# A hybrid decoder layer on one core: writing a recurrence head's level preparation in one piece

## Chip, cores and metric

The kernel runs on one core of a Trainium2 chip. The metric is the device time of one execution in microseconds (us). Engines are named as in the profile: PE (TensorE matmuls), PEld (its weight loads), DVE (VectorE), ACT (ScalarE), POOL (GpSimd), SP (the queue that issues most DMAs).

## The reference, cut to what matters

One decoder layer over 2048 tokens of width 1024: modulated RMSNorm, one input projection, two head groups, an output projection, then a gated MLP with a short convolution. Head group A is sliding-window attention. Head group B, which the change touches, is a gated linear recurrence with 4 heads of key and value width 128:

```
f = lower_bound + (1 - lower_bound) * sigmoid(f_logit);  k = 1 - f;  q = silu(q)
S_t = diag(f_t) S_{t-1} + k_t i_t^T,   o_t = S_t^T q_t
```

In chunkwise form the score of query t and key s in a chunk is the sum over the key dimension of q_t times the product of f from s+1 to t times k_s.

## The kernel before

**Stages.** The mixer works through four groups g of 512 tokens (`GT`), the later stages through the output projection, the up projection and the down projection; the down projection starts at about 1970 us. In a group the four recurrence heads are handled in two pairs, (0, 1) and (2, 3). For each pair `hg_scores` (L781 to L884) builds the decayed scores AT of four chunks of 128 tokens, and `hg_state` (L886) carries the state. In the trace, `a_q` is a head's query tile, `K` its key tile, `f` its forget gate, all 128 x 512 float32, keys on partitions and tokens along the row.

**Levels.** A score between tokens that first differ in bit w of their index is a product of a scaled query and a scaled key. So `hg_scores` goes through widths w = 1, 2, 4, ... 64. `scaled(h, w)` (L819) multiplies the second halves of the query blocks by `tots` (for w = 1: f itself) and the first halves of the key blocks by it, and folds `tots` by two: three DVE instructions, written in place. Widths 0, 1 and 2 are done without matmuls over blocks: a DVE product (`raw`, L811, L816, L839) is split into a high part (ACT, to `ph` or `p`) and a low part (POOL, to `pl` or `p`), and much later summed by matmuls with a matrix of ones (`lv_d`, `lv<-ph`, `lv<-p`). From w = 4 on PE makes a block of scores (`lv<-a_q,K`) in a PSUM bank of the tag "hg" (two banks), and DVE or ACT merges it into AT.

**Preparation before the change.** For both heads of a pair: raw0 = q k, its split, q = q f, raw1 = odd q times even k, its split. Then for both heads: `scaled(h, 1)`, raw2, its split. Then for both heads: `scaled(h, 2)`. Then the loop over w = 4 to 64, again over both heads in each turn.

**Buffers.** The six `raw` tiles of a pair come from one tag, "ln", with `bufs=3`: three buffers, handed out in the order in which the tiles are written in the program. In the old order they are raw0 and raw1 of the first head, raw0 and raw1 of the second, raw2 of the first, raw2 of the second. A buffer is free again when both the ACT and the POOL instruction of its split are done.

**Order on the engines.** The program is fully unrolled. ACT is pinned to program order through `hg_scores` and `hg_state`. DVE, POOL, PE and SP are not pinned there: before the launch a planner places each engine's instructions by expected readiness, the earlier in the program the higher the priority. On the chip each engine then takes its list strictly in order. During the pair (0, 1) PE also has the projection `ps_i` of this group (`proj_i`), during the pair (2, 3) the attention projections `ps_k`, `ps_q` (`proj_attn`), so that level matmuls stand in PE's list between projection matmuls.

**Names in the rows.** `w_..h` and `w_..l` are high and low parts of projection weights, split by ACT and by DVE or POOL; `ada` and `part` belong to a sum over the conditioning weights that DVE does on the side; `s_q` is the sigmoid of a query, and POOL's `a_q<-a_q,s_q` makes silu. All rows show line L46, the helper through which every instruction passes.

Of the kernel before, what the change touches and what calls it, by code (L numbers as in the profile page):

```python
# [8 lines left out]
F32 = mybir.dt.float32  # L9
# [4 lines left out]
ALU = mybir.AluOpType  # L14
# [4 lines left out]
P = 128  # L19
# [6 lines left out]
GT = 512  # L26
# [27 lines left out]
def kernel(ctx, tc, x, c, ada_w, ada_b, mix_norm_g, w_in, b_in, attn_sinks, attn_out_g,  # L54
# [3 lines left out]
    V, S, G, TE, SY = (InOrder(tc, e) for e in (nc.vector, nc.scalar, nc.gpsimd, nc.tensor, nc.sync))  # L58
# [105 lines left out]
    def split(src, hi, lo, hi_eng=None, lo_eng=None):  # L164

        if hi_eng is V:
            V.tensor_copy(out=hi, in_=src)
        else:
            S.activation(hi, src, AF.Copy)
        (lo_eng or V).tensor_tensor(out=lo, in0=src, in1=hi.bitcast(F32), op=ALU.subtract)  # L170
# [59 lines left out]
    with ExitStack() as mx:  # L230
# [334 lines left out]
        for e in range(2):  # L565

            hp, op = slice(e * 64, e * 64 + 64), slice(64 - e * 64, 128 - e * 64)
# [4 lines left out]
        mt = hgp.enter_context(tc.tile_pool(name="mt", bufs=2, side="right", reuse_waits="tile"))  # L572
# [16 lines left out]
        for g in range(NG):  # L589
# [169 lines left out]
            qs, ks, fs, ats, on, kts, tots = {}, {}, {}, {}, {}, {}, {}  # L759
# [21 lines left out]
            def hg_scores(hs_):  # L781
# [11 lines left out]
                def sums(h, hi, lo, label):  # L793
# [4 lines left out]
                    TE.matmul(ps, lhsT=ones_r, rhs=lo, start=False, stop=True)  # L798
                    return ps


                ph, pl, p1 = {}, {}, {}
                for h in hs_:
# [11 lines left out]
                    raw = mt.tile([P, GT], F32, tag="ln", bufs=3, name=f"raw1_{g}_{h}")[:, 0:GT // 2]  # L815
                    V.tensor_tensor(out=raw, in0=q2[:, :, 1], in1=k2[:, :, 0], op=ALU.mult)  # L816
                    split(raw, p1[h][:, 0, :], p1[h][:, 1, :], lo_eng=G)

                def scaled(h, w):  # L819

                    q4 = qs[h].rearrange("p (n a h) -> p n a h", a=2, h=w)
                    k4 = ks[h].rearrange("p (n a h) -> p n a h", a=2, h=w)
                    t3 = tots[h].rearrange("p (n a) -> p n a", a=2)
                    ns = GT // (2 * w)
                    V.tensor_tensor(out=q4[:, :, 1, :], in0=q4[:, :, 1, :],
                                    in1=t3[:, :, 0:1].broadcast_to([P, ns, w]), op=ALU.mult)
                    V.tensor_tensor(out=k4[:, :, 0, :], in0=k4[:, :, 0, :],
                                    in1=t3[:, :, 1:2].broadcast_to([P, ns, w]), op=ALU.mult)
                    nt = mt.tile([P, ns], F32, tag=f"tot{w}", name=f"tot_{g}_{h}_{w}")
                    V.tensor_tensor(out=nt, in0=t3[:, :, 0], in1=t3[:, :, 1], op=ALU.mult)  # L830
                    tots[h] = nt

                for h in hs_:
                    scaled(h, 1)
                    q4 = qs[h].rearrange("p (n a h) -> p n a h", a=2, h=2)[:, :, 1, :]
                    k4 = ks[h].rearrange("p (n a h) -> p n a h", a=2, h=2)[:, :, 0, :]
                    raw = mt.tile([P, GT], F32, tag="ln", bufs=3, name=f"raw2_{g}_{h}")
                    full4 = [P, GT // 4, 2, 2]
                    V.tensor_tensor(out=raw.rearrange("p (n t s) -> p n t s", t=2, s=2),  # L839
                                    in0=q4.unsqueeze(3).broadcast_to(full4), in1=k4.unsqueeze(2).broadcast_to(full4),  # L840
                                    op=ALU.mult)
                    split(raw, ph[h][1], pl[h][1], lo_eng=G)
                for h in hs_:
                    scaled(h, 2)
                w = 4
                while w <= 64:
                    for h in hs_:
                        q, k, at = qs[h], ks[h], ats[h]
                        nm = f"{g}_{h}"
                        if w <= 16:  # L850
                            ps = full(h, w)
                        else:
                            ps = bank(f"lv_{nm}_{w}", "hg").rearrange("p (a b) -> p a b", a=4)
                            for cc in range(4):
                                for s0 in range(0, P, 2 * w):
                                    a0 = cc * P + s0
                                    TE.matmul(ps[s0:s0 + w, cc, s0 + w:s0 + 2 * w], lhsT=k[:, a0:a0 + w],
                                              rhs=q[:, a0 + w:a0 + 2 * w], start=True, stop=True)
                        scaled(h, w)
                        if w <= 16:  # L860
                            V.copy_predicated(at, bc4(lev[w]), ps)
                        else:
                            for s0 in range(0, P, 2 * w):
                                S.activation(at[s0:s0 + w, :, s0 + w:s0 + 2 * w],
                                             ps[s0:s0 + w, :, s0 + w:s0 + 2 * w], AF.Copy)
                    w *= 2
# [79 lines left out]
            weights(g, "i", 0, ahead=1)  # L946
            pin(True, S)
            hg_scores((0, 1))
            i_tok = proj_i()
            hg_state((0, 1))  # L950
# [9 lines left out]
            weights(g, "k", 0)  # L960
            pin(True, S)
            hg_scores((2, 3))
            hg_state((2, 3))
            pin(False, S)
# [561 lines left out]
```

## Time and profile before

| | |
|---|---|
| median of 3 runs | 2494.3 us (2492.16 to 2494.49) |
| the profiled execution | 2490.66 us |
| its span, first to last instruction | 2488.9 us |
| PE busy | 2323.8 us, 93% of the span |
| DVE busy | 1911.0 us, 77% |
| ACT busy | 1055.6 us, 42% |
| POOL busy | 919.4 us, 37% |
| mean granted TensorE clock | 0.974 |

Busy times are of the whole span. A row of the timeline gives the start in us from the span's start, the duration in us, engine, line, operation, output<-inputs, shape and type, the number of instructions merged into the row, and in brackets the engine's idle time before it and what ended it.

### The profile page before, as it was taken

How to read it: one execution, taken by the hardware profiler on the slowest of the kernel's cores; microseconds unless marked ns; L12 is line 12 of the kernel's file. 1: busy time of each engine (PE TensorE's matmuls, PEld its weight loads, DVE VectorE, ACT ScalarE, POOL GpSimd, SP SyncE). 2: the span in 40 equal slices, each digit the busy share in tenths (PEclk: the TensorE clock that was granted, in tenths of full speed). 3: DMA queues.
4: the chain of work that ended last, by engine and by line, in shares of the span. 5: the costliest groups of instructions: out<-in, count | busy, mean ns of one | idle time of the engine just before them, and what ended most of it. 6: DMA issues, size and time to landing. Idle time of an engine off the chain costs nothing.

```text
span 2488.9 us, 35680 instructions
## 1 busy us (share of the span) xinstructions
PE 2323.8 (93%) x13369; PEld 2010.0 (81%) x13369; DVE 1911.0 (77%) x2743; ACT 1055.6 (42%) x1776; POOL 919.4 (37%) x743
## 2 busy tenths in 40 slices
PE   5889898998989899999999999999999789997997
PEld 4778786887878688887888887788888679997997
DVE  8888778888876876568888888788877776676665
ACT  3336434623733454454333334333332344455443
POOL 6222212222322221225757564788888410011000
PEclk8999999999999999999999999999999889998999
DMA  7343233323322247664444245455454577687776
GB/s 213 90 119 98 81 91 96 94 69 101 95 68 85 85 159 246 204 204 131 139 129 144 93 140 189 158 159 163 161 157 166 199 260 218 211 283 263 260 243 203
DMA packets 337304, 389.90 MB, mean 157 GB/s; under 512 B 14069, under 2 KB 258763, under 8 KB 337131
## 3 DMA queue, kind: packets, MB, share of 16 engines
q1 hardware_dynamic: 326571, 347.25, 44.8%
q0 software_dynamic: 10560, 40.37, 4.4%
q8 instruction: 105, 1.72, 0.3%
q14 instruction: 68, 0.56, 0.1%
HBM read 293.71 MB, written 93.86 MB: 156 GB/s over the span
## 4 chain that ended last, share of the span: by engine, by line
PE 66%; DVE 13%; DMA 7%; POOL 6%; issue 5%; ACT 2%; SPq 0%; DVEq 0%; ACTq 0%; POOLq 0%
PE ps_u L46 24%; PE ps_d L46 15%; PE ps_o L46 5%; PE lv L46 3%; PE ps_hg L46 3%; PE ps_hq L46 2%; PE ps_hf L46 2%; PE ps_i L46 2%; PE att_o L46 2%; DVE ada L46 2%; DMA ada<-in_ada_w_dram 1%; POOL s L46 1%; PE ps_q L46 1%; DVE raw L46 1%; POOL sm L46 1%
## 5 line engine op out<-in xcount | busy, mean ns | idle before, releaser
L46 DVE TENSOR_TENSOR Tl<-da,Th 128x896 fp32r<-128x896 f32 x176 | 201.5, 1154 | 119.9 <-ACT Th L46 119.8
L46 ACT ACTIVATE Th<-da 128x896 fp32r<-128x896 f32 x176 | 166.5, 949 | 194.6 <-PE ps_d L46 161.5
L46 DVE SCALAR_TENSOR_TENSOR cc<-ub,cols,cc 128x1024 f32<-128x1024 f32 x88 | 153.4, 1743 | 14.3 <-ACT cc L46 12.0
L46 PE MATMUL lv<-a_q,K 128*128 128x128 f32 (+2 forms) x768 | 78.6, 262 | 43.8 <-DVE K L46 39.7
L46 PEld LDWEIGHTS lv<-a_q,K 128*128 128x128 f32 (+2 forms) x768 | 70.4, 173 | 56.5 <-DVE K L46 28.2
L46 DVE TENSOR_TENSOR cc<-cc,v 128x1024 f32<-128x1024 f32 x44 | 64.9, 1476 | 44.5 <-ACT cc L46 44.5
L46 POOL TENSOR_TENSOR s<-wu_0r,s 128x512 f32<-128x512 f32 x44 | 59.3, 1347 | 107.4 <-DVE ws_0l L46 14.8
L46 ACT ACTIVATE cc<-cc 128x1024 f32<-128x1024 f32 x44 | 46.7, 1060 | 122.5 <-DVE cc L46 122.5
L46 POOL TENSOR_TENSOR s<-wu_1r 128x512 f32<-128x512 f32 x44 | 68.8, 1563 | 70.1 <-DVE t_T4l L46 15.8
L46 POOL TENSOR_TENSOR wu_1r<-wu_0r,wu_1r 128x512 f32<-128x512 f32 x44 | 92.9, 2111 | 3.1
L46 POOL MEMSET AT<- 128x512 f32 x16 | 8.5, 532 | 230.3 <-PE ho L46 208.3
L46 POOL TENSOR_TENSOR pl<-raw,ph 128x512 fp32r<-128x512 f32 x32 | 44.6, 1395 | 101.2 <-ACT ph L46 101.2
L46 POOL TENSOR_SCALAR rv_d<-ssd 128x2 f32<-128x2 f32 x8 | 1.5, 192 | 208.5 <-DVE ssd L46 208.5
L46 POOL TENSOR_TENSOR S_0l<-Sr,S_0h 128x512 fp32r<-128x512 f32 x1 | 2.6, 2601 | 201.9 <-ACT S_0h L46 201.9
L46 POOL TENSOR_TENSOR s<-s,wu_0r 128x512 f32<-128x512 f32 x44 | 73.7, 1674 | 0.0
L46 DVE TENSOR_TENSOR v<-ps_u,v 128x512 f32<-128x512 f32 x88 | 60.4, 686 | 15.5 <-PE ps_u L46 12.2
L46 DVE COPY_PREDICATED AT<-lev,lv 128x512 f32<-128x512 uint32 (+1 forms) x96 | 70.0, 729 | 2.4 <-PE lv L46 1.1
L46 DVE TENSOR_TENSOR ada<-ada,cond 128x1024 f32<-128x1024 f32 (+1 forms) x37 | 54.9, 1483 | 15.3 <-DMA ada<-in_ada_w_dram 13.9
L46 ACT ACTIVATE cc<-ub,cols 128x1024 f32<-128x1024 f32 x44 | 54.5, 1240 | 24.7 <-DVE ub L46 24.7
L46 DVE TENSOR_TENSOR a_q<-a_q,tot 128x256 f32<-128x256 f32 x96 | 52.8, 550 | 9.5 <-PE lv L46 8.5
L46 DVE TENSOR_TENSOR ub<-ps_u,u 128x512 f32<-128x512 f32 x88 | 60.0, 682 | 0.1
L46 DVE TENSOR_TENSOR ot<-ps_o,gate 128x512 f32<-128x512 f32 x32 | 22.0, 688 | 46.6 <-PE ps_o L46 45.6
(2138 smaller groups left out, 9178.8 us busy)
## 6 DMA issues: line engine op xcount, KB each, us to landing
da<-act_d SPq DMA_DIRECT2D x176, 448.0 KB, 4.0
wu_0r<-in_w_up_dram SPq DMA_DIRECT2D x44, 512.0 KB, 4.5
wu_1r<-in_w_up_dram SPq DMA_DIRECT2D x44, 512.0 KB
act_d<-cc POOLq DMA_DIRECT2D x44, 512.0 KB, 4.0
ada<-in_ada_w_dram SPq DMA_DIRECT2D x40, 512.0 KB, 6.4
act_d<-sm POOLq DMA_DIRECT2D x22, 768.0 KB, 4.2
x<-in_x_dram SPq DMA_DIRECT2D x26, 512.0 KB, 5.8
Sr<-wc_d SPq DMA_DIRECT2D x18, 512.0 KB, 7.1
```

What stands on the lines that cost most here:

```text
L46: ins = fn(*args, **kwargs)
```

## The change

`scaled` is defined ahead of the first loop, and three loops over the heads of the pair become one. Each head goes through raw0, q f, raw1, `scaled(h, 1)`, raw2, `scaled(h, 2)` before the other head begins. The instructions, their shapes, tiles and buffers stay as they are, and so does the loop from w = 4 on. The `raw` tiles are now written in the order raw0, raw1, raw2 of the first head, then raw0, raw1, raw2 of the second.

```diff
+                def scaled(h, w):
...
                 for h in hs_:
                     G.memset(ats[h], 0.0)
...
                     V.tensor_tensor(out=raw, in0=q2[:, :, 1], in1=k2[:, :, 0], op=ALU.mult)
                     split(raw, p1[h][:, 0, :], p1[h][:, 1, :], lo_eng=G)
-
-                def scaled(h, w):
...
-                for h in hs_:
                     scaled(h, 1)
                     q4 = qs[h].rearrange("p (n a h) -> p n a h", a=2, h=2)[:, :, 1, :]
                     k4 = ks[h].rearrange("p (n a h) -> p n a h", a=2, h=2)[:, :, 0, :]
...
                     split(raw, ph[h][1], pl[h][1], lo_eng=G)
-                for h in hs_:
                     scaled(h, 2)
                 w = 4
                 while w <= 64:
```

## Rows read from the trace of the kernel before

**Rows 1.** The page: the span, and busy time by engine.
```profile
span 2488.9 us, 35680 instructions
PE 2323.8 (93%) x13369; PEld 2010.0 (81%) x13369; DVE 1911.0 (77%) x2743; ACT 1055.6 (42%) x1776; POOL 919.4 (37%) x743
```
**Rows 2.** Waits of PE: total us, times, longest us.
```profile
PE lv L46 <- DVE K L46: 39.7, 7, 7.4
...
PE lv L46 <- DVE AT L46: 5.2, 6, 1.2
```
**Rows 3.** Busy us by engine, clock and DMA in windows: the sum over the eight pair stages.
```profile
sum 538.00, PE 482.71 PEld 417.99 DVE 449.95 ACT 175.91 POOL 125.02; mean PE 60.34 PEld 52.25 DVE 56.24 ACT 21.99 POOL 15.63
```
**Rows 4.** Timeline of PE, pair (0, 1) of group 1.
```profile
305.10 3.44 PE L46 MATMUL lv<-a_q,K 128*128 128x128 f32 x16 [4.22 <-DVE K L46]
```
**Rows 5.** Timeline of DVE, the same pair.
```profile
288.08 0.42 DVE L46 TENSOR_TENSOR K<-K,f 128x256 f32<-128x256 f32 x1
...
293.99 1.23 DVE L46 TENSOR_TENSOR w_i_0l<-w_i_0r,w_i_0h 128x1024 fp32r<-128x1024 f32 x1 [2.87 <-ACT w_i_0h L46]
295.13 1.57 DVE L46 TENSOR_SCALAR f<-f,omc,lbc 128x512 f32<-128x512 f32 x1
296.74 0.84 DVE L46 TENSOR_SCALAR K<-f 128x512 f32<-128x512 f32 x1
...
302.62 1.48 DVE L46 TENSOR_TENSOR a_q<-a_q,tot 128x256 f32<-128x256 f32 x1
```
**Rows 6.** Timeline of POOL, the same pair.
```profile
289.75 1.36 POOL L46 TENSOR_TENSOR a_q<-a_q,s_q 128x512 f32<-128x512 f32 x1 [8.18 <-ACT s_q L46]
295.13 1.29 POOL L46 TENSOR_TENSOR pl<-raw,ph 128x512 fp32r<-128x512 f32 x1 [4.03 <-ACT ph L46]
...
302.39 1.44 POOL L46 TENSOR_TENSOR pl<-raw,ph 128x512 fp32r<-128x512 f32 x1
```
**Rows 7.** Instructions on `raw`, `tot` and `f`: duration ns min/median/max, starts, shapes.
```profile
L46 DVE TENSOR_TENSOR raw<-a_q,K x48: 411/679/2891, 88.8 to 815.4; 128x512 f32<-128x512 f32 x32, 128x256 f32<-128x256 f32 x16
...
L46 DVE TENSOR_TENSOR tot<-tot x96: 150/184/1290, 92.9 to 802.1; 128x128 f32<-128x128 f32 x16, 128x64 f32<-128x64 f32 x16, 128x32 f32<-128x32 f32 x16, 128x16 f32<-128x16 f32 x16
L46 DVE TENSOR_TENSOR a_q<-a_q,tot x96: 403/424/2556, 101.5 to 831.6; 128x256 f32<-128x256 f32 x96
...
L46 DVE TENSOR_SCALAR f<-f,omc,lbc x16: 534/544/1571, 86.2 to 798.4; 128x512 f32<-128x512 f32 x16
```
**Rows 8.** Timeline of DVE, pair (2, 3) of group 1.
```profile
353.18 2.89 DVE L46 TENSOR_TENSOR raw<-a_q,K 128x512 f32<-128x512 f32 x1
...
358.06 1.67 DVE L46 TENSOR_TENSOR tot<-tot 128x16 f32<-128x16 f32 x3
...
364.56 1.23 DVE L46 TENSOR_TENSOR ada<-ada,cond 128x1024 f32<-128x1024 f32 x1 [3.96 <-DMA ada<-in_ada_w_dram]
...
374.85 1.23 DVE L46 TENSOR_TENSOR ada<-ada,cond 128x1024 f32<-128x1024 f32 x1 [1.19 <-DMA ada<-in_ada_w_dram]
...
376.65 1.12 DVE L46 TENSOR_TENSOR ada<-ada 128x512 f32<-128x512 f32 x1
...
383.48 1.48 DVE L46 TENSOR_TENSOR a_q<-a_q,tot 128x256 f32<-128x256 f32 x1
```
**Rows 9.** Timeline of POOL, the same pair.
```profile
352.92 2.60 POOL L46 TENSOR_TENSOR w_k_0l<-w_k_0r,w_k_0h 128x1024 fp32r<-128x1024 f32 x1 [3.75 <-ACT w_k_0h L46]
...
375.43 1.79 POOL L46 TENSOR_TENSOR pl<-raw,ph 128x512 fp32r<-128x512 f32 x1 [16.13 <-ACT ph L46]
```
**Rows 10.** Timeline of PE, the same pair.
```profile
386.05 3.75 PE L46 MATMUL lv<-a_q,K 128*128 128x128 f32 x16 [6.97 <-DVE K L46]
...
390.70 1.05 PE L46 MATMUL lv<-a_q,K 128*128 128x128 f32 x8
```
**Rows 11.** Two windows at low granted clock: busy us by engine, clock, DMA share, GB/s.
```profile
304.63:308.04 3.41, 2.94 (x14) 2.94 (x15) 3.41 (x8) 0.63 (x1) 1.39 (x1) 0.50 0.00 0
383.14:389.96 6.82, 3.91 (x17) 3.91 (x18) 5.70 (x11) 2.17 (x3) 2.95 (x3) 0.50 0.66 164
```

More of the change, by code (lines that the diff above doesn't have):

```diff
@@ L799, in sums @@
                     return ps
+                def scaled(h, w):
+                    q4 = qs[h].rearrange("p (n a h) -> p n a h", a=2, h=w)
+                    k4 = ks[h].rearrange("p (n a h) -> p n a h", a=2, h=w)
+                    t3 = tots[h].rearrange("p (n a) -> p n a", a=2)
+                    ns = GT // (2 * w)
+                    V.tensor_tensor(out=q4[:, :, 1, :], in0=q4[:, :, 1, :],
+                                    in1=t3[:, :, 0:1].broadcast_to([P, ns, w]), op=ALU.mult)
+                    V.tensor_tensor(out=k4[:, :, 0, :], in0=k4[:, :, 0, :],
+                                    in1=t3[:, :, 1:2].broadcast_to([P, ns, w]), op=ALU.mult)
+                    nt = mt.tile([P, ns], F32, tag=f"tot{w}", name=f"tot_{g}_{h}_{w}")
+                    V.tensor_tensor(out=nt, in0=t3[:, :, 0], in1=t3[:, :, 1], op=ALU.mult)
+                    tots[h] = nt
                 ph, pl, p1 = {}, {}, {}
@@ L817, in hg_scores @@
                     split(raw, p1[h][:, 0, :], p1[h][:, 1, :], lo_eng=G)
-                def scaled(h, w):
[L821 to L831, printed above, removed]
-                for h in hs_:
                     scaled(h, 1)
```

## The prediction, on record before the result was known

> **What bounds the kernel now.** I read the page first. PE is busy for 93% of the span and DVE for 77% [rows 1], so the question in each stage is when PE has to stop. The edit touches only `hg_scores`, which runs eight times before 850 us. Windows over those eight stages give 538 us with 482.7 us of PE at work [rows 3]: at most 55 us are there to be won, 2.2% of the span. The list of PE's waits says where most of that is: PE stood 39.7 us, 7 times, up to 7.4 us, ahead of a level matmul `lv` for a key tile K from DVE [rows 2]. That is one stop in each of seven stages, ahead of the first head's first level.
>
> In the timeline the reader is to see what such a stop is. PE does projection matmuls without a break, reaches `lv` in its list and stands 4.22 us (pair 0, 1) or 6.97 us (pair 2, 3) [rows 4, 10]. More projection work was there, but behind `lv` in a fixed list. So a stop measures how far DVE lags behind the place that the planner gave the matmul. It does not measure how long DVE's chain is.
>
> Where does DVE lag? In the pair (0, 1) five instructions ahead of K are too long, from f (1.57 us for a median of 0.54) to a_q by tot (1.48 for 0.42) [rows 5, 7]: by 1.03, 0.41, 1.05, 0.52 and 1.06 us, together 4.07, for a stop of 4.22. They are those under which POOL works: POOL's `pl` from 302.39 to 303.83 holds the a_q of 302.62 until 304.10 [rows 5, 6]. In the pair (2, 3) four such instructions, from the `ada` of 1.12 to the a_q of 1.48 [rows 8], are too long by 0.43, 0.88, 0.53 and 1.06, together 2.9 us. The rest of 6.97 is the DMA of `ada`: 1.19 us of waiting at 374.85, and by subtraction 2.9 of the 3.96 us at 364.56 [rows 8].
>
> **The change, part by part.** Nothing is removed or added: the same instructions, no DMA among them, so nothing is moved past a transfer in SP's or POOL's queue. Three things move.
>
> (1) *The first head's third product comes early.* In the old order raw2 of the first head is the fifth tile on three buffers and waits for the split of raw1. The trace shows it: its last factor was done at 288.50, and DVE later idled 2.87 us ahead of 293.99 [rows 5] without doing it. Now it is the third tile and waits for nothing. With it go `scaled(h, 2)`, together 0.68 + 2 x 0.42 = 1.5 us of DVE [rows 7], then the first level matmuls of that head and about as much DVE work behind them (two scalings and a merge). It falls into idle time of DVE, 2.87 us there and 3.96 us in the other pair [rows 5, 8], so it costs nothing; without that cover it is 3 us per stage.
>
> (2) *The second head's first product comes late.* It is now the fourth tile and waits until POOL is through with `pl` of the first head. In the pair (0, 1) that is 296.42 [rows 6], while the K that it needs is only made at 296.74 [rows 5]: no cost. In the pair (2, 3) it is 377.22 [rows 9], since ACT's splits are pinned behind those of the weights. From there the second head needs two raws and a q by f of full width, one raw of half width and four scalings: 3 x 0.68 + 5 x 0.42 = 4.1 us. In the old order one half raw, two full ones and six scalings stood between that point and both heads' first levels: 2 x 0.68 + 7 x 0.42 = 4.3 us. That is even.
>
> (3) *PE gets two places to wait instead of one.* The planner will list the first head's `lv` as soon as it expects its K, some 10 us earlier in the pair (0, 1) and 20 us earlier in the pair (2, 3), and the second head's by itself.
>
> The early place. In the pair (0, 1), POOL's a_q of 1.36 us [rows 6] lies over the moved instructions: a stop of 0 to 1.3 us; I take 1.0. In the pair (2, 3), POOL's `w_k_0l` holds raw0 for 2.89 us, 2.2 too long [rows 8, 9], and three tots take 1.67 for 3 x 0.18 [rows 7, 8], 1.1 too long: 3.3 us, bounds 0 (the planner lists the matmul later) and 3.3. Around the old stops, with PE idle, the granted clock was 0.50, the lower level, for 3.41 or 6.82 us [rows 11], and the 16 matmuls behind them took 3.44 and 3.75 us, while 8 took 1.05 later [rows 4, 10]. So a second stop of that kind costs up to 1.5 us more; I take 1.5 in the pair (2, 3), none in the other.
>
> The late place. In the pair (0, 1) five POOL instructions lie ahead of the second head's K as before, so the 4.07 stays; with three of the first head in a row I take 4.5, bounds 2.5 (planned waits for buffers take up some) and 6.0, the POOL time itself, 1.29 to 1.44 us for the first and last of the five [rows 6]. In the pair (2, 3) the 2.9 stays, and of the 4.1 us behind `ada` 1.3 are left, since PE itself is then 4.8 us later: 4.2, bounds 2.9 and 7.
>
> The rows show 4.07 us held out of 6.0 us of POOL's work. The Trainium skill (SBUF — State Buffer, "Who interferes with whom") states a full lock: a VectorE instruction with two SBUF inputs and a GpSimd instruction that reads SBUF exclude each other, and the later one waits for the whole of the other. By that rule, with DVE at such work throughout, the late stop is 6.0 and not 4.5, and the sum below 4.5 us higher. It agrees with the single 1.48 us row; that DVE is never elsewhere is not seen here.
>
> What goes. Six waits for AT, 5.2 us [rows 2], lie between the levels; with one level done early I let 0.8 per stage go.
>
> **Sum.** Pair (0, 1), groups 1 to 3: 1.0 + 4.5 - 4.2 - 0.8 = +0.5 each. Pair (2, 3), groups 1 to 3: 3.3 + 1.5 + 4.2 - 7.0 - 0.8 = +1.2 each. Group 0, where three heads' inputs come together: 0, between -3 and +3. Together 1.5 + 3.6 = +5.1; I round down to +4.5, as 1.5 for the clock is an upper bound. On the profiled execution (2490.7 us: its span and 1.8 around it) that is 2495.2. The median of the runs lies 3.6 above that execution: 2494.3 + 4.5 = 2498.8.
>
> **Rivals.**
> *The gain is real (faster).* The early matmul is listed late enough to cost nothing, and the second head's K is met with the moved 1.5 us out of the way. Seven stops are shorter by 1.5 us and most waits for AT go: -10.5 - 3.5 = -14, 2480. For it: DVE's idle time is there [rows 5, 8]. Against it: (2) puts as much DVE work behind the same POOL instruction, and the stops follow POOL's time, which stays.
> *Two full stops (slower).* The early stop comes and the late one does not shrink, because what lags behind `ada` is fed by PE and shifts with it. Then +1.3 in three pairs (0, 1) and 3.3 + 1.5 - 0.8 = +4.0 in four pairs (2, 3): +20, 2514. It decides where the late stop of a pair (2, 3) stays above 6 us. Against it: more than half of the 6.97 is DMA [rows 8], whose issue does not wait for PE's level matmuls.
> *Nothing happens.* The planner orders by readiness, and DVE's list comes out as it was: 2494. Against it: the buffer that kept raw2 back is now free.
>
> **How the numbers follow.** The forecast (stops split, not shortened) gets 0.47, the gain 0.25, two full stops 0.20, nothing 0.08. Within 0.2%, 5 us, is about what a measurement of this kernel cannot tell from no change. The forecast's own range is 2491 to 2505, for each stop is uncertain by 1 to 2 us; of its 0.47 some 0.30 lies within 5 us, 0.15 above, 0.02 below. With the rivals: faster 0.27, within 0.38, slower 0.35. The range over all leaves a tenth out on either side: 2484 to 2511, into both rivals but not to their ends.
>
> **What the new profile would show.** The first head's three raws stand together, and its first level of 8 matmuls stands 10 or 20 us ahead of the second head's. I am right if PE waits for K twice per stage, near 1.0 and 4.5 us in the pairs (0, 1) and near 3.3 and 4.2 us in the pairs (2, 3), over the kernel some 3 x 5.5 + 3 x 7.5 + 6 = 45 us where it was 39.7. I am wrong if the early wait is missing (then the gain), if POOL's `pl` no longer holds DVE up, or if the planner shifts the attention projections so that PE stops elsewhere.

## The result, and the profile after

The changed kernel takes 2523.2 us (median of 4 runs, 2520.2 to 2524.6) where the kernel before takes 2493.3 beside it: a ratio of 1.0117, 95% interval 1.0104 to 1.0129. That is 29.9 us slower; 4.5 were forecast, and the range ended at 2511.

The page of the changed kernel, its span and busy times:

```profile
span 2522.8 us, 35676 instructions
...
PE 2340.4 (93%) x13369; PEld 2022.3 (80%) x13369; DVE 1924.8 (76%) x2743; ACT 1058.8 (42%) x1778; POOL 917.1 (36%) x743
```

Against [rows 1] the span of the profiled execution is longer by 33.9 us, in two halves. PE stands for 182.4 us (span less busy) where it stood for 165.1: 17.3 more. And the same 13,369 matmuls keep it busy for 16.6 us more. They ran slower: the trace has 165 us at the granted clock of 0.50, the lower of its two levels, before 131. Of PE's busy time 117.8 us lie there, before 87.2. At half the clock, half of that time is extra: 15.3 us more than before, nearly all of the 16.6.

PE's waits (total us, times, longest us):

```profile
PE lv L46 <- DVE K L46: 34.9, 7, 8.0
PE lv L46 <- DVE tot L46: 20.4, 5, 5.5
...
PE sc L46 <- DVE on L46: 9.2, 5, 3.3
...
PE lv L46 <- DVE AT L46: 0.9, 1, 0.9
```

Where there were seven stops of 39.7 us [rows 2] there are twelve of 55.3. The waits for AT between the levels went, as forecast (5.2 to 0.9). So PE's idle time ahead of `lv` grew by 11.3 us. The other 6.0 of the 17.3 lie elsewhere. Grown is `sc<-on`, attention's first scores, of which the kernel before had

```profile
PE sc L46 <- DVE on L46: 1.3, 1, 1.3
```

All waits ahead of `sc` together grew by 7.0 us; ahead of the projection `ps_q` 2.8 are new, ahead of `ps_i` 4.4 went.

The eight stages, cut at the last output matmul `ho` of each pair, so that those of the pairs (0, 1) of groups 1 to 3 hold the attention part ahead of them too (length, busy us of PE, PEld, DVE, ACT, POOL, granted clock, DMA share, GB/s):

```profile
80.00:144.60 64.60, 53.88 (x381) 49.71 (x380) 52.74 (x109) 15.45 (x27) 15.24 (x14) 0.87 0.23 66
144.60:219.80 75.20, 65.59 (x359) 54.10 (x359) 64.19 (x117) 27.20 (x45) 17.18 (x14) 0.93 0.34 98
219.80:359.90 140.10, 126.85 (x849) 111.77 (x848) 113.66 (x242) 69.82 (x167) 32.61 (x37) 0.96 0.30 91
359.90:436.80 76.90, 69.34 (x386) 57.64 (x384) 60.06 (x102) 29.31 (x48) 19.31 (x17) 0.96 0.25 74
436.80:575.80 139.00, 128.79 (x872) 113.30 (x871) 113.52 (x240) 68.07 (x169) 31.09 (x37) 0.98 0.29 89
575.80:656.10 80.30, 71.77 (x398) 59.62 (x396) 66.08 (x116) 29.20 (x48) 19.16 (x17) 0.94 0.31 90
656.10:800.30 144.20, 131.27 (x861) 115.75 (x860) 108.98 (x226) 71.02 (x171) 30.85 (x37) 0.94 0.24 75
800.30:884.60 84.30, 73.05 (x396) 60.06 (x395) 68.30 (x120) 29.32 (x48) 19.22 (x16) 0.94 0.28 82
```

Cut the same way, the kernel before has 56.0, 68.7, 137.5, 77.0, 135.4, 75.5, 142.2 and 77.4; its group 0 reads:

```profile
80.00:136.00 56.00, 48.27 (x380) 44.19 (x378) 50.80 (x104) 15.26 (x27) 16.73 (x14) 0.97 0.24 67
136.00:204.70 68.70, 60.69 (x345) 49.41 (x344) 61.69 (x115) 27.09 (x45) 15.96 (x14) 0.95 0.33 94
```

The differences are +8.6, +6.5 in group 0, then +2.6, -0.1, +3.6, +4.8, +2.0 and +6.9. Group 0, forecast at nothing, has 15 of the 35; the pairs (2, 3) of groups 2 and 3 have 12. Of the 11.3 us by which PE's idle time ahead of `lv` grew, 9.2 lie in group 0 and 2.1 in groups 1 to 3 together.

The stops in PE's timeline:

```profile
93.77 2.05 PE L46 MATMUL lv<-a_q,K 128*128 128x128 f32 x8 [2.77 <-DVE tot L46]
...
111.98 3.78 PE L46 MATMUL lv<-a_q,K 128*128 128x128 f32 x16 [4.73 <-DVE K L46]
...
161.06 1.43 PE L46 MATMUL lv<-a_q,K 128*128 128x128 f32 x8 [3.74 <-DVE tot L46]
...
188.18 3.78 PE L46 MATMUL lv<-a_q,K 128*128 128x128 f32 x16 [5.30 <-DVE K L46]
...
309.38 1.16 PE L46 MATMUL lv<-a_q,K 128*128 128x128 f32 x8 [1.03 <-DVE K L46]
...
323.01 3.75 PE L46 MATMUL lv<-a_q,K 128*128 128x128 f32 x16 [4.21 <-DVE tot L46]
...
405.84 3.78 PE L46 MATMUL lv<-a_q,K 128*128 128x128 f32 x16 [6.87 <-DVE K L46]
```

In group 0 the kernel before had one such stop:

```profile
171.92 1.43 PE L46 MATMUL lv<-a_q,K 128*128 128x128 f32 x5 [6.08 <-DVE K L46]
```

In the pair (0, 1) of group 1 the stop of 4.22 us [rows 4] became two, 1.03 and 4.21, nearly the 1.0 and 4.5 of the forecast. In the pair (2, 3) the early stop of 3.3 is not there, and the late one, forecast at 4.2, is 6.87; in groups 2 and 3 it is 7.96 and 7.94 (before: 6.97, 6.45 and 7.43). The reader sees why in DVE's timeline ahead of 405.84:

```profile
394.45 1.22 DVE L46 TENSOR_TENSOR raw<-a_q,K 128x512 f32<-128x512 f32 x1 [1.19 <-POOL pl L46]
395.70 1.67 DVE L46 TENSOR_TENSOR a_q<-a_q,f 128x512 f32<-128x512 f32 x1
397.47 1.33 DVE L46 TENSOR_TENSOR raw<-a_q,K 128x256 f32<-128x256 f32 x1
...
400.41 2.76 DVE L46 TENSOR_TENSOR raw<-a_q,K 128x512 f32<-128x512 f32 x1
...
403.98 1.47 DVE L46 TENSOR_TENSOR a_q<-a_q,tot 128x256 f32<-128x256 f32 x1
```

and in POOL's:

```profile
393.06 1.36 POOL L46 TENSOR_TENSOR pl<-raw,ph 128x512 fp32r<-128x512 f32 x1 [16.11 <-ACT ph L46]
394.38 0.74 POOL L46 TENSOR_TENSOR p<-raw,p 128x256 fp32r<-128x256 f32 x1
395.07 3.45 POOL L46 TENSOR_TENSOR pl<-raw,ph 128x512 fp32r<-128x512 f32 x2
399.33 0.85 POOL L46 TENSOR_TENSOR p<-raw,p 128x256 fp32r<-128x256 f32 x1 [0.81 <-ACT p L46]
400.28 2.34 POOL L46 TENSOR_TENSOR w_v_0l<-w_v_0r,w_v_0h 128x1024 fp32r<-128x1024 f32 x1
403.90 1.26 POOL L46 TENSOR_TENSOR pl<-raw,ph 128x512 fp32r<-128x512 f32 x1 [1.29 <-ACT ph L46]
```

The second head's first product waits 1.19 us for POOL's `pl`, which had waited 16.11 us for ACT. From there its whole preparation runs beside POOL's. By the medians of their kinds (0.68 us at full width, 0.42 at half, [rows 7]) the five DVE instructions are too long by 0.54, 0.99, 0.91, 2.08 and 1.05: 5.57, and with the wait 6.76, for a stop of 6.87. In the kernel before, that first product began at 369.57, 5.9 us ahead of POOL's `pl` [rows 9].

### The profile page after: what moved, and what is told of

Read it like the earlier page. It is cut to its first block, busy times and chain, and to the rows that moved or that the text cites. A ratio compares the mean times of both kernels' runs of the same rounds, so it can differ in the third digit from the quotient of the medians.

```text
span 2522.8 us, 35676 instructions
## 1 busy us (share of the span) xinstructions
PE 2340.4 (93%) x13369; PEld 2022.3 (80%) x13369; DVE 1924.8 (76%) x2743; ACT 1058.8 (42%) x1778; POOL 917.1 (36%) x743
## 4 chain that ended last, share of the span: by engine, by line
PE 57%; DVE 15%; POOL 12%; issue 7%; DMA 6%; ACT 2%; SPq 0%; DVEq 0%; POOLq 0%; ACTq 0%
PE ps_u L46 16%; PE ps_d L46 15%; PE ps_o L46 7%; PE lv L46 3%; POOL s L46 3%; PE ps_hg L46 3%; PE ps_i L46 2%; POOL sm L46 2%; PE att_o L46 2%; PE ps_hq L46 2%; PE ps_hf L46 2%; DVE ada L46 2%; POOL wu_1r L46 2%; DVE raw L46 2%; PE ps_q L46 1%
## 5 line engine op out<-in xcount | busy, mean ns | idle before, releaser
L46 PE MATMUL lv<-a_q,K 128*128 128x128 f32 (+2 forms) x768 | 84.9, 273 | 55.3 <-DVE K L46 34.9
L46 PEld LDWEIGHTS lv<-a_q,K 128*128 128x128 f32 (+2 forms) x768 | 76.9, 184 | 68.2 <-DVE K L46 38.3
L46 DVE TENSOR_TENSOR v<-ps_u,v 128x512 f32<-128x512 f32 x88 | 60.4, 686 | 15.4 <-PE ps_u L46 12.1
L46 ACT ACTIVATE cc<-ub,cols 128x1024 f32<-128x1024 f32 x44 | 54.6, 1240 | 25.2 <-DVE ub L46 24.0
L46 DVE TENSOR_TENSOR a_q<-a_q,tot 128x256 f32<-128x256 f32 x96 | 46.2, 481 | 22.0 <-PE lv L46 21.6
L46 DVE TENSOR_TENSOR ot<-ps_o,gate 128x512 f32<-128x512 f32 x32 | 21.9, 687 | 52.3 <-PE ps_o L46 46.1
```

The costliest lines, as they stand in the source:

```text
L46: ins = fn(*args, **kwargs)
```

## The experiments

The runs weigh theories against each other. Two at first. **A**: the loss comes from the second place at which PE stops, and from the low clock behind it. **B**: it comes from the second head's preparation, which starts later and runs under POOL. After the first four runs **C**, POOL's hold on DVE is why K is late at all, and **D**, it only shifts a lag with other roots.

In the tables, idle is span less PE's busy time; stops is PE's idle time ahead of level matmuls (`lv`); pace, in the text, is the difference in PE's busy time; held is the time by which DVE's instructions on `raw`, `a_q`, `K`, `tot` and `f` up to 950 us exceed the median of their kind in the kernel before, added up from the trace. The kernel before has 2493 us, idle 165.1, busy 2323.8, stops 44.9, held 46.1; the changed one 2523, 182.4, 2340.4, 56.2, 53.8.

### Runs 1 to 4: two places, or a late second head

Run 1, on the changed kernel, puts the second head's first level first in PE's list:

```diff
-                    for h in hs_:
+                    for h in (hs_[::-1] if w == 4 else hs_):
```

> The changed kernel, but at the first level the second head's matmuls are allotted before the first head's, so that the first head's early place in PE's list is gone (in PE's list the two heads' first levels stand side by side again in all eight stages, as in the kernel before, while DVE still prepares one head after the other). Theory A (the loss comes from the second place at which PE has to stop, and from the low clock that follows it): one stop per stage again, low-clock time back to some 55 us, and a median of 2493 to 2503. Theory B (the loss comes from the second head's preparation, which starts later and runs under POOL's work): the late stops of 7 to 8 us stay in the pairs (2, 3) and the median stays at 2512 to 2524.

Run 2, on the changed kernel (`raw0` of the second head in a buffer of its own):

```diff
-raw = mt.tile([P, GT], F32, tag="ln", bufs=3, name=f"raw0_{g}_{h}")
+raw = mt.tile([P, GT], F32, name=f"raw0_{g}_{h}",
+              **(dict(tag="lx", bufs=1) if h == hs_[1] else dict(tag="ln", bufs=3)))
```

> The changed kernel with one more buffer of 2 KB a partition, in which the second head's first product goes, so that it need not wait until POOL is through with the first head's lo part. PE's list still has the first head's first level early. Theory A (two stops): the early stops stay, at most the late ones shrink by a third, 2510 to 2523. Theory B (the second head is late): the wait of DVE for POOL's pl ahead of the second head's first product is gone, the late stops in the pairs (2, 3) fall from 7 to 8 us to about 4, and the median falls to 2490 to 2505.

Run 3 does the same for `raw2` of the first head (`hs_[0]`) in the kernel before.

> The kernel before with one more buffer of 2 KB, in which the first head's third product goes, so that it need not wait for the split of another. The source stays step by step for both heads; the planner may now do the first head's third product early, as the change does, without pushing the second head's first product behind POOL's pl. Theory A (two stops): the first head's first level is listed early and PE stops twice in each stage, so 2505 to 2520. Theory B (the second head is late): the second head is in time, 2485 to 2497.

Run 4, on the kernel before:

```diff
                     split(raw, ph[h][1], pl[h][1], lo_eng=G)
-                for h in hs_:
                     scaled(h, 2)
```

> The kernel before with only the last of the two moved steps joined: the second scaling of a head follows its third product at once, while the first two products of both heads stay ahead as they were. In PE's list the first head's first level then stands only 8 to 16 matmul groups ahead of the second head's, where the whole change makes it 70 to 92. Theory A (two stops): a split stop, but the two places are some 3 us apart, so a half of the loss at most, 2496 to 2512. Theory B (the second head is late): its first product is where it was, so 2488 to 2499.

| run | median us | ratio to before, interval | idle | PE busy | stops | held |
|---|---|---|---|---|---|---|
| 1 | 2511.3 | 1.0065 (1.0052 to 1.0077) | 173.0 | 2336.6 | 45.2 | 49.5 |
| 2 | 2531.2 | 1.0148 (1.0132 to 1.0163) | 189.4 | 2338.1 | 64.4 | 54.6 |
| 3 | 2531.5 | 1.0146 (1.0132 to 1.0160) | 187.1 | 2340.5 | 64.6 | 53.2 |
| 4 | 2507.9 | 1.0050 (1.0038 to 1.0063) | 165.1 | 2338.7 | 36.2 | 47.5 |

Neither theory holds as posed. Run 1 brings the stops back to those of before, but only 12 of the 30 us, and the late stops of 6.9 to 7.4 us in the pairs (2, 3) stay, as B had it, whose range its time misses by 0.7 us: A is a part at most. Runs 2 and 3 take away the wait for the buffer and get slower, out of the ranges of A and of B. They come out alike, too: 2531.2 and 2531.5 us, with early stops of 3.0 and 3.6 or 2.9 and 3.6 us in group 0 and late ones of 9.06 and 9.10 in the pair (2, 3) of group 1. So with one buffer more even the old source order loses as much as the new one and more; its wait for a buffer had kept the kernel before from it. In run 2, pair (2, 3) of group 1, DVE's timeline ends like this:

```profile
396.43 2.32 DVE L46 TENSOR_TENSOR ada<-ada,cond 128x1024 f32<-128x1024 f32 x1 [0.78 <-DMA ada<-in_ada_w_dram]
398.67 2.56 DVE L46 TENSOR_TENSOR a_q<-a_q,tot 128x256 f32<-128x256 f32 x1
```

and POOL's beside it:

```profile
397.62 3.32 POOL L46 TENSOR_TENSOR w_v_0l<-w_v_0r,w_v_0h 128x1024 fp32r<-128x1024 f32 x1
```

The first product no longer waits, but an `ada` now stands inside the second head's chain, and POOL's weight holds the instruction behind it: a stop of 9.06 us. Run 4 falls into A's range for another reason: PE idles no longer than before, its stops are 8.7 us shorter, and the loss is PE's pace (busy +14.9).

### Runs 5 to 12: POOL's work moved to DVE

The edits, each on both kernels: (lo) the levels' lo subtractions; (sig) the product of a query or gate with its sigmoid; (w) the lo parts of the weights v, k, hq 0 and hg 2.

```diff
-                    split(raw, ph[h][0], pl[h][0], lo_eng=G)
+                    split(raw, ph[h][0], pl[h][0])
...
-                G.tensor_tensor(out=a, in0=a, in1=sg, op=ALU.mult)
+                V.tensor_tensor(out=a, in0=a, in1=sg, op=ALU.mult)
...
-            split(r, w[0], w[1], lo_eng=low(nm))
+            split(r, w[0], w[1], lo_eng=V)
```

> The kernel before with the lo subtractions of the levels' three products (two of 128x512 and one of 128x256 per head) on DVE instead of POOL. DVE gets some 16 x (0.68 + 0.68 + 0.43) = 28.6 us more work, and POOL no longer holds DVE there. Theory C (POOL's hold on DVE, which the planner does not book, is why K comes late): the level stops of 45 us fall to 25 or less, and the median to 2470 to 2490. Theory D (the lag has other roots, the hold only shifts it): stops of 40 us or more, 2492 to 2510.

> The changed kernel with the same lo subtractions on DVE. Theory C: the second head's products no longer run under POOL, the level stops of 56 us fall to 30 or less, and the distance to the kernel before with the same edit is under 12 us where it was 30. Theory D: the distance stays at 20 to 35 us, since two places to stop and the low clock behind them remain. Theory A of the first runs (two stops) stands with D here.

> As the kernel before with the levels' lo subtractions on DVE, and besides the product of a query or gate with its sigmoid, and the lo parts of the weights v, k, hq 0 and hg 2, moved from POOL to DVE: POOL keeps no instruction of two SBUF inputs and full width in the stages of the levels. DVE gets some 80 us more in all. Theory C: no DVE instruction of the levels is held any more, level stops of 15 us or less; the time is 2470 to 2495, depending on what the added DVE work costs elsewhere. Theory D: stops of 30 us or more remain.

> The changed kernel with the same POOL work moved to DVE. Theory C: level stops of 15 us or less, and at most 8 us between this kernel and the kernel before with the same edit. Theory D, or theory A (two stops): 15 to 35 us between them, with early stops still there ahead of the first head's first level.

> The kernel before with the other half of the POOL work moved to DVE: the product of a query or gate with its sigmoid and the lo parts of the weights v, k, hq 0 and hg 2; the levels' lo subtractions stay on POOL. If each half of POOL's work adds its share (theory C): level stops between 45 and 11 us, near 28, and 2468 to 2486.

> The changed kernel with that same other half moved to DVE, the levels' lo subtractions on POOL. With the run before it this completes a table of two halves. If the levels' own lo subtractions under the second head's products are what the change loses by (theory B in its new form), the distance to the kernel before with the same edit stays at 20 to 35 us. If the other half is what it loses by, as the 23 us between the two kernels with only the lo subtractions moved suggest, the distance is under 10 us.

> The kernel before with the levels' lo subtractions and the products with the sigmoid on DVE, the lo parts of the weights v, k, hq 0 and hg 2 still on POOL. Between the kernel with the lo subtractions alone moved (2459) and the one with all moved (2444): 2444 to 2460.

> The changed kernel with the same edit. If POOL's products with the sigmoid (which lie over the first head's moved instructions) are what remained of the loss, the distance to the kernel before with the same edit falls from 23 us to under 8; if the lo parts of the weights are (2.3 to 2.6 us each, one ahead of the first head's early level and one over the second head's third product in the pairs (2, 3)), it stays at 12 to 25 us.

| runs | moved | old order: us, interval of the ratio | new order | new - old | idle | PE busy | stops | held |
|---|---|---|---|---|---|---|---|---|
| 5, 6 | lo | 2459.2, 0.9846 to 0.9873 | 2482.2, 0.9929 to 0.9956 | +23.1 | 136.6, 143.8 | 2320.2, 2337.8 | 17.0, 22.8 | 21.9, 18.8 |
| 9, 10 | sig, w | 2476.1, 0.9919 to 0.9944 | 2492.1, 0.9979 to 0.9998 | +16.1 | 145.9, 159.8 | 2327.8, 2331.1 | 32.9, 47.6 | 29.9, 31.6 |
| 11, 12 | lo, sig | 2477.2, 0.9925 to 0.9952 | 2467.1, 0.9877 to 0.9904 | -10.1 | 144.4, 136.6 | 2331.0, 2329.0 | 15.0, 19.3 | 10.1, 11.0 |
| 7, 8 | all | 2444.2, 0.9788 to 0.9814 | 2443.6, 0.9784 to 0.9811 | -0.6 | 127.0, 117.4 | 2320.3, 2323.1 | 11.4, 9.0 | 0, 0 |

With all of it moved the two orders take the same time, and both are 2% faster than the kernel before: these are the fastest versions. The instructions on `raw` in run 7 (ns, least, median and greatest; the greatest was 2891 [rows 7]):

```profile
L46 DVE TENSOR_TENSOR raw<-a_q,K x48: 417/684/691, 90.9 to 773.3; 128x512 f32<-128x512 f32 x32, 128x256 f32<-128x256 f32 x16
```

At this end C holds and D falls: no hold, hardly a late K, and no loss by the new order. But POOL's lateness is taken away together with its hold, since no `pl` is left to wait for, and these runs don't tell the two apart. Nor is the table smooth between the ends. Runs 5 and 6 miss C's "under 12" and lie in the 20 to 35 of D and A: 23 us apart with no more hold in the one than in the other. There the new order still has early stops (2.87 and 3.74 us in group 0, 1.0 in the pairs (0, 1)), 7 us more idle time and 17.6 us of pace. Runs 5, 7 and 8 are faster than expected (2459 for 2470 at the least, 2444 for 2470). Run 9 came as expected. Runs 9 and 10 are 16 us apart, between the two cases posed (20 to 35, under 10), and in run 10 the stops are 47.6 though a third of the hold is gone: stops do not follow the hold one to one. Run 12 was to come within 8 us of run 11 and is 10 us faster. Run 11 should have lain below run 5 and is 18 us above it, 10.8 of them pace; why is not settled. PE's list is made anew for each edit, and while such an 18 is unexplained, a difference of 10 to 20 us between two kernels of this table says little by itself.

### Runs 13 to 16: the clock, and the stages

Run 13 is the changed kernel unchanged. Runs 14 to 16 take the new order under a condition, else the old one:

```diff
-                for h in hs_:
+                if g > 0:            # run 15: hs_[0] == 0; run 16: hs_[0] == 2
+                    for h in hs_:
...
```

> The changed kernel once more, word for word, for a second trace. If the low clock in it is a matter of the kernel's own order, the second trace has again some 165 us of low clock (131 in the kernel before) and its periods stand at the same stages; if it is a matter of the single execution, the time at the low clock differs by 10 us or more from the first trace and stands elsewhere.

> The new order in groups 1 to 3 only, the old one in group 0. By the two traces the stages of group 0 grew by 15 of the 34 us. If the losses of the stages add up, some 17 of the 30 us remain: 2506 to 2516. If group 0 costs nothing, as was predicted, 2519 to 2527.

> The new order in the pairs (0, 1) of all groups only. By the two traces these stages grew by 8.7, 2.6, 3.6 and 2.0 us, together 17 of 34: if they add up, 2505 to 2514. By the sum of the prediction they cost 0.5 each, 2494 to 2498.

> The new order in the pairs (2, 3) of all groups only. By the two traces these stages grew by 6.4, -0.1, 4.7 and 7.0 us, together 18 of 34: if they add up, 2505 to 2514, with late level stops of 7 to 8 us that have not shrunk and early ones only in group 0. By the sum of the prediction 1.2 each, 2495 to 2500.

| run | median us | ratio, interval | idle | PE busy | stops |
|---|---|---|---|---|---|
| 13 | 2521.5 | 1.0109 (1.0085 to 1.0134) | 178.6 | 2335.9 | 55.5 |
| 14 | 2524.5 | 1.0122 (1.0108 to 1.0136) | 186.8 | 2334.4 | 55.9 |
| 15 | 2502.7 | 1.0031 (1.0019 to 1.0043) | 169.2 | 2328.7 | 55.2 |
| 16 | 2509.9 | 1.0064 (1.0050 to 1.0079) | 173.6 | 2336.2 | 47.6 |

One window at the low clock in the first trace of the changed kernel:

```profile
404.10:410.93 6.83, 5.09 (x20) 4.80 (x21) 5.10 (x9) 1.12 (x2) 1.07 (x1) 0.50 0.24 71
```

and the same place in the second:

```profile
404.41:411.24 6.83, 5.11 (x20) 4.82 (x21) 5.09 (x9) 1.10 (x2) 1.05 (x1) 0.50 0.23 68
```

The first nine low-clock periods after 90 us recur, each 0.3 us later; from 619 us on some differ in length, and the whole is 156 us instead of 165. So the pace belongs to the kernel's order, up to some 5 of the 16.6 us that one execution makes. In each of the 20 traces PE's busy time, less half of what lies at the granted clock of 0.50, is 2279 to 2285 us: but for these 6 us the differences in pace are the clock, in all these kernels.

The pairs (0, 1) alone cost 10 us, a little less than expected, the pairs (2, 3) alone 17, as expected: together 27 of 30. In run 15 the pair (0, 1) of group 0 grew by 7.4 us, and those of groups 1 to 3 by -0.4, 0.5 and 1.6, near the 0.5 forecast; in run 16 the pair (2, 3) of group 0 grew by 9.8, the others by -0.4, 4.2 and 7.6. So group 0, put at nothing, costs 17 us in these two runs. It does not add up with the rest: without it the loss is still 31 and not some 17, as if group 0 cost nothing. In run 14 the `ada` stood in the pairs (2, 3) of groups 1 and 2 (in the changed kernel not in group 1), with a stop of 9.7 us in the one and two of 5.0 and 6.4 in the other.

### Runs 17 and 18: when POOL comes

On both kernels ACT is held to program order only from the state part on:

```diff
-            pin(True, S)
             hg_scores((0, 1))
+            pin(True, S)
...
-            pin(True, S)
             hg_scores((2, 3))
+            pin(True, S)
```

> The kernel before with ACT no longer held to program order in the level scores (it stays so in the state part). ACT's high parts of the products then need not stand behind those of the weights, and POOL's lo parts start some us earlier. If that only moves POOL's hold to other DVE instructions, 2485 to 2505 with level stops of 35 to 50 us.

> The changed kernel with the same edit. Its second head's first product waits for POOL's first lo part, which waited 12 to 16 us for ACT's high part, and then the whole preparation of the second head ran under POOL. In PE's list the second head's first level now stands 25 to 45 rows behind the first head's in the pairs (2, 3) and in group 0, where it was 80 to 90. If this lateness is what made the change lose in those stages, the late stops there fall from 7 or 8 us to 5 or less, and the distance to the kernel before with the same edit to 0 to 15 us. If the hold alone matters, whenever it comes, it stays at 20 us or more.

| run | order | median us | ratio, interval | idle | PE busy | stops | held |
|---|---|---|---|---|---|---|---|
| 17 | old | 2524.0 | 1.0121 (1.0106 to 1.0137) | 180.0 | 2343.2 | 42.5 | 48.2 |
| 18 | new | 2509.9 | 1.0067 (1.0055 to 1.0080) | 174.2 | 2333.8 | 42.7 | 42.1 |

The sign turns: with ACT free the new order is 14.2 us faster than the old one, and shorter in each of the eight stages (1.2 to 3.4 us). The level stops are not what makes it so, 42.5 and 42.7 us: 9.4 us are pace, 5.8 idle time elsewhere. The late stops of the pairs (2, 3), expected at 5 or less, are 3.86, 5.00, 7.26 and 6.05. Both lose to the kernel before, run 17 by far more than expected, for a reason beside the levels, in PE's waits:

```profile
PE sc L46 <- DVE comb L46: 20.4, 4, 6.7
```

It was 3.4 us in the kernel before, and it is 20.8 in run 18. In run 18, pair (2, 3) of group 1, DVE's timeline reads:

```profile
373.93 0.68 DVE L46 TENSOR_TENSOR raw<-a_q,K 128x512 f32<-128x512 f32 x1
...
376.77 0.41 DVE L46 TENSOR_TENSOR raw<-a_q,K 128x256 f32<-128x256 f32 x1
...
380.20 0.68 DVE L46 TENSOR_TENSOR raw<-a_q,K 128x512 f32<-128x512 f32 x1
```

and POOL's:

```profile
375.35 1.35 POOL L46 TENSOR_TENSOR pl<-raw,ph 128x512 fp32r<-128x512 f32 x1 [7.80 <-ACT ph L46]
```

POOL's lo parts come one at a time, between the two heads. The second head's first product waits for nothing, and none of its three is held. Even so PE stands at that place:

```profile
382.30 2.06 PE L46 MATMUL lv<-a_q,K 128*128 128x128 f32 x9 [5.00 <-DVE tot L46]
```

Two other instructions, a `tot` and a scaling of K, are too long by 1.1 and 0.5 us; what makes up the rest of the 5.00 is not settled. So POOL coming earlier does not do away with the late stop.

## Why the prediction was wrong

**What bounds the kernel** was read rightly: the stops at `lv` are DVE's lag, and POOL's work is most of the lag. Runs 7 and 8 take that work away and the stops fall from 45 to about 10 us.

**Which terms failed.** The 33.9 us of the two profiles are 9.2 of level stops in group 0, 2.1 of level stops in groups 1 to 3, 6.0 of idle time at other places and 16.6 of pace. The sum had nothing, 0.6, nothing and 4.5. So three terms failed: group 0, the other places, and the clock. The stops of groups 1 to 3 came near their forecast, but by luck: in the pairs (2, 3) the early ones, put at 3.3, did not come, and the late ones were 2.7 to 3.8 us longer than the 4.2 forecast.

**Group 0**, taken at nothing within 3 and without a reason from its rows, grew by 15 us, through early stops of 2.77 and 3.74 and late ones of 4.73 and 5.30, where there had been one of 6.08. Its late places have the same `pl`, which waits 12 and 22 us there. Its early stops are perhaps POOL's only in part: with POOL's work moved to DVE, run 8 still has 1.99 and 1.03.

**The clock** was mis-sized: three times 1.5 us where PE's busy time grew by 16.6 (12.1 in the second trace). Not only long stops were followed by low clock, as run 4 shows, with shorter stops and 14.9 us of pace; which gaps bring it is not settled.

**The other places.** One sign of being wrong was that PE stops elsewhere; it came in part, with the 7.0 us ahead of attention's scores and the 2.8 ahead of its projection, less the 4.4 that went.

**(1) The first head's third product early** costs nothing: right in the pairs (0, 1) of groups 1 to 3, which grew by -0.4 to 1.6 us in run 15. Its raws stand together, and in groups 1 and 2 the early stop was 1.03 (forecast 1.0). For the whole kernel it isn't shown: run 3, whose only edit lets that product come early in the kernel before, loses 37 us.

**(2) "That is even" failed as a mechanism.** I counted the DVE work behind POOL's `pl` at its bare durations, 4.1 us against 4.3, and asked only when the buffer comes free. But what comes after `pl` is the rest of POOL's work, and in the new order it lies over the whole second head. From 394.45 to the K at 405.78 the second head took 11.3 us, and the held time grew from 46.1 to 53.8. Freeing the buffer (run 2) didn't help. With POOL coming earlier (run 18) the held time is 42.1 against 48.2 and the sign turned, though not by the level stops.

**(3) The late place.** For the pairs (0, 1) the 4.5 holds (4.21, 4.19 and 5.48). For the pairs (2, 3) I took 4.2, with a bound of 7, since I held 2.9 us for POOL's and let 1.3 of DMA's 4.1 stand; with PE 4.8 us later, by my own working, none of it was left, so the 4.2 doesn't come out of its rows. In group 1 no `ada` was left in the pair, yet the stop was 6.87, and the rows above put 6.76 of it down to POOL. My "Against it" for the rival of two full stops, that more than half was DMA, was therefore no argument: DMA's part went and POOL's took its place. That rival (2514) was the nearest, and the late stops stayed above 6 us, as it had it. Yet its 20 us are not those measured: its early stop of 3.3 us came in the pair (2, 3) of group 0 alone (3.74), and most of the loss lies in the three terms above. Near in number, it was right in part only.

The other two rivals fell at once: stops did not shorten (the gain), and PE's list did change (nothing happens).

The Trainium skill (SBUF — State Buffer, "Who interferes with whom") states that a VectorE instruction with two SBUF inputs and a GpSimd instruction that reads SBUF exclude each other, the later one waiting for the whole of the other. Here the `raw` of 400.41, 0.13 us behind the start of POOL's `w_v_0l`, ended at 403.17, 0.55 us after it (402.62), so that one row agrees. The sum by that rule, 4.5 us higher, would not have saved the forecast: it put the excess in the pairs (0, 1), whose late stops were 4.21, 4.19 and 5.48.

**What stays open**: whether POOL's hold or its lateness is what the new order loses by; the 23 us between runs 5 and 6, where the hold is the same; what brings the low clock, half of the loss; and how much of the 30 us is the new order's own and how much that of the one list which the planner made from it, since edits that should add up do not (run 14).

## What to carry to other kernels

When a piece of work is moved, ask not only when its inputs and buffers are ready at the new place but which other engine's work will lie over it there: a count of bare durations misses an engine that holds them (4.1 us counted, 11.3 taken). A stage that looks different from the others is priced from its own rows and not put at nothing. A sum that comes near is looked through term by term, for two wrong terms can cancel. Where a stop has two causes, removing one may only make room for the other. If two engines hold each other up, moving the work of one to the other can be worth more than its order: here 2% won, where the reordering lost 1.2%.

## What the runs showed that was not expected

In run 7 DVE does 95 instructions more and is busy for less time than in the kernel before (1911.0 us [rows 1]); POOL goes from 919.4 to 773.4:

```profile
PE 2320.3 (95%) x13369; PEld 2005.3 (82%) x13369; DVE 1902.4 (78%) x2838; ACT 1060.6 (43%) x1780; POOL 773.4 (32%) x648
```

What DVE took over cost it less than what it had stood held. POOL takes longer beside DVE too: its `pl` takes 1.26 us at the least, but 3.45 for two at 395.07. And two stops of nearly one length, 4.22 us [rows 4] and 4.21 us at the same place of the changed kernel, go with low clock of 3.41 us [rows 11] and of 6.83 us (322.18 to 329.01).
